# New places for the weight sums, sample rows by way of scratch, and a new order of issue in a two-part attention layer

## The chip, the cores and the metric

The kernel runs on one core of one Trainium2 chip. Its time is the device time of one execution in microseconds (us); the kernel before has a median of 773.05 us over three runs. One execution of it was also profiled, instruction by instruction, and that trace is what the text reads.

A core has five engines that run side by side, each with its own instruction queue in order: PE (TensorE, the matmuls; PEld is its weight load), DVE (VectorE), ACT (ScalarE), POOL (GpSimd) and SP (SyncE). In this kernel every transfer (DMA) is issued by SP.

## What is computed

One layer of a streaming encoder, in float32, for a prompt of 1024 frames and a sample of 32 frames that has 512 cached ones before it:

```python
hn = rmsnorm(h, g_pre)
qa, ka, va, ga, qb, kb, vb, gb = split(hn @ w_in)
oa = band_attention(qa, ka, va, bias)          # 8 heads x 64: softmax over a band of 576 frames
ob = stick_breaking(qb, kb, vb)                # 8 heads x 64: strictly causal, running products
y = concat(oa * silu(ga), ob * silu(gb)) @ w_out
h = h + rmsnorm(y, g_post)
h = h + sigmoid(h @ w_ple_gate) * (p @ w_ple)
```

Outputs are `h` of the prompt and of the sample, and the keys and values: of the prompt (the last 512 frames for A, all for B) and of the sample (32 frames x 8 heads x 64, four tensors: A keys, A values, B keys, B values).

## The kernel before, in words

**Work.** Each product takes its operands as a high and a low part in a rounded format, three matmuls for one. The heads go in pairs, in the order A0, B0, A1, B1, A2, B2, A3, B3 (number n = 0 to 7). Beside the attention of pair n (two heads of eight row blocks: scores, weights, transposed weights, product with the values) stand the projections q, k and v of pair n + 1, and beside the last pair all eight gate projections. Pairs n = 2, 3, 6 and 7 (A1, B1, A3, B3) also carry a sample attention over two pairs of heads (`with_sample`, `SAMPLE_AT`). Then come the small product `ple`, and the last two products, `w_out` and `w_ple_gate`. These two use a scheme of seven products of half-size blocks (`ORDER`) in place of eight, which needs sums of weight blocks.

**The sums.** `sum_weights(w, kt)` makes the sums for one of four slices of a weight: it loads four 128x512 blocks (tiles oB... for `w_out`, gB... for `w_ple_gate`, three buffers), makes four subtractions or additions in two halves each on POOL (8 instructions), and stores four results to `sum_dr`, a scratch tensor in DRAM. `SUMS_AT` says beside which pair two slices stand, `SUMS_STEP` after how many steps of that pair. The sums are read back from `sum_dr` when the attention is over.

**Sample rows.** `keys_out` transposes a pair's keys in 32x32 squares into a tile (ktA, ktB), and `values_out` does so for values (vtA, vtB). The sample's part of that tile is 128 x 32: four groups of 32 partitions, each holding 32 features of the 32 frames. `sample_rows` writes each group to the output with a transfer of its own: four for each pair's keys and four for its values, 64 in all, each of 32 runs of 128 bytes. For values the same tile also goes to the scratch `vs_dr[ab][p]` by `then(out, last)`; the sample attention reads its new values there (tile vn).

**The order.** Nothing is issued as it is written. A recorder collects all operations with their dependences, and `order` simulates the engines with costs from `cost`, finds for each operation how late it can be (`latest`, its due time), and simulates again with the due times as ranks; the instruction streams come out of that. The rank is `o.due + 10 * o.shift` (ns) in the last round. The shifts stand in two tables written out by hand: `AHEAD_OF` by engine and name of the written tile, `AHEAD_AT` by stage as well (pair n is stage n + 1). `PASSES` says how often due times and simulation are repeated. For SP, `ISSUE` is the time of an issue; `DMA_START`, `DMA_DONE`, `DMA_RATE`, `DMA_MARGIN` give a transfer's course. In `simulate`, SP may have 1900 pieces (rows of a transfer) under way (`AWAY`) and waits in the model when there would be more. `later` marks output transfers with a lower key, which counts in the first simulation alone. `rec.hold` keeps the buffers of a sum from being taken before the matmul that was recorded last.

All recorded operations have one line in the profile, L780, from which they are emitted; names of tiles tell them apart.

Of the kernel before, what the change touches and what calls it, by code (L numbers as in the profile page):

```python
# [10 lines left out]
AF = mybir.ActivationFunctionType  # L11
ALU = mybir.AluOpType

P = 128
D = 1024
SEQ = 1024
NS = 32
# [11 lines left out]
    ('ACT', 'L'): -809, ('ACT', 'Qfs'): -495, ('ACT', 'S'): -671, ('ACT', 'be'): 45,  # L29
    ('ACT', 'gT'): 1145, ('ACT', 'junk'): -1222, ('ACT', 'o'): 225, ('ACT', 'oT'): -1406,  # L30
    ('ACT', 'om'): -82, ('ACT', 'ot'): -967, ('ACT', 'p'): -874, ('ACT', 'pleo'): -1053,
    ('ACT', 'sgg'): 65, ('ACT', 'stq'): -314, ('ACT', 'stv'): -824, ('ACT', 'v'): 55,
    ('ACT', 'wTh'): -117, ('ACT', 'whS'): 246, ('ACT', 'whs'): 933, ('ACT', 'x'): -696,
    ('ACT', 'xS'): -616, ('DVE', 'Kl'): -588, ('DVE', 'L'): 544, ('DVE', 'S'): -85,
    ('DVE', 'Vl'): -913, ('DVE', 'cc'): -493, ('DVE', 'diags'): -1253, ('DVE', 'g'): 212,
    ('DVE', 'h'): -1097, ('DVE', 'hnl'): 570, ('DVE', 'lg'): 343, ('DVE', 'om'): -53,
    ('DVE', 'ot'): -267, ('DVE', 'over'): 483, ('DVE', 'sgg'): -356, ('DVE', 'sq'): 277,
    ('DVE', 'stats'): -1190, ('DVE', 'uu'): 246, ('DVE', 'v'): -653, ('DVE', 'vx'): -722,
    ('DVE', 'w'): -1469, ('DVE', 'wTl'): 37, ('DVE', 'wl'): 652, ('DVE', 'wlS'): -1002,
# [3 lines left out]
    ('POOL', 'be'): 196, ('POOL', 'gT'): 309, ('POOL', 'o'): -123, ('POOL', 'ogg'): 890,  # L43
    ('POOL', 'om'): 197, ('POOL', 'rs'): -497, ('POOL', 's'): -1046, ('POOL', 'sgg'): 929,
# [4 lines left out]
}  # L49
AHEAD_AT = {  # L50
    (0, 'ACT', 'pleo'): 1195, (0, 'ACT', 'sq'): 1380, (0, 'ACT', 'stk'): -1095, (0, 'ACT', 'v'): 1160,
    (0, 'DVE', 'hnl'): -45, (0, 'DVE', 'rb'): 799, (0, 'DVE', 'sq'): 461, (0, 'DVE', 'x'): 572,
# [3 lines left out]
    (2, 'ACT', 'be'): -135, (2, 'ACT', 'om'): 146, (2, 'ACT', 'stk'): -313, (2, 'ACT', 'stv'): 933,  # L56
    (2, 'ACT', 'v'): -818, (2, 'ACT', 'wTh'): 315, (2, 'ACT', 'wh'): -172, (2, 'DVE', 'S'): 534,
    (2, 'DVE', 'om'): 779, (2, 'DVE', 'wTl'): -209, (2, 'PE', 'PV'): 241, (2, 'PE', 'S'): 63,
    (2, 'PE', 'mm'): 48, (2, 'PE', 'ptw'): 89, (2, 'POOL', 'be'): -1200, (2, 'SP', 'kl'): 504,
    (2, 'SP', 'swap'): 262, (3, 'ACT', 'be'): 80, (3, 'ACT', 'om'): 256, (3, 'ACT', 'stk'): 956,  # L60
    (3, 'ACT', 'wh'): -21, (3, 'ACT', 'whs'): -356, (3, 'DVE', 'om'): -326, (3, 'DVE', 'ot'): -819,
# [3 lines left out]
    (4, 'ACT', 'om'): -35, (4, 'ACT', 'wTh'): -365, (4, 'ACT', 'whs'): -1064, (4, 'DVE', 'S'): -89,  # L65
    (4, 'DVE', 'Ss'): 1254, (4, 'DVE', 'ot'): 307, (4, 'DVE', 'wTl'): -134, (4, 'PE', 'S'): 77,
    (4, 'PE', 'ptw'): 56, (4, 'PE', 'ptws'): -349, (4, 'POOL', 'ksS'): -959, (4, 'POOL', 'om'): 162,
    (4, 'POOL', 'w'): -151, (4, 'POOL', 'wl'): 1076, (4, 'SP', 'Kcs'): 477, (4, 'SP', 'be'): -112,
    (4, 'SP', 'o'): -577, (4, 'SP', 'wr'): -890, (5, 'ACT', 'be'): -546, (5, 'ACT', 'kd'): -484,
    (5, 'ACT', 'stk'): 1450, (5, 'ACT', 'wTh'): -482, (5, 'DVE', 'S'): -110, (5, 'DVE', 'om'): -127,  # L70
# [3 lines left out]
    (6, 'ACT', 'L'): 734, (6, 'ACT', 'be'): -459, (6, 'ACT', 'kd'): 409, (6, 'ACT', 'stv'): 1412,  # L74
# [4 lines left out]
    (7, 'ACT', 'om'): 64, (7, 'ACT', 'stk'): -573, (7, 'ACT', 'wTh'): -208, (7, 'DVE', 'Kcs'): 660,  # L79
# [6 lines left out]
    (8, 'POOL', 'ogg'): -1077, (8, 'POOL', 'om'): 190, (8, 'POOL', 'sgg'): -350, (8, 'POOL', 'w'): 324,  # L86
# [3 lines left out]
    (10, 'POOL', 'r'): 153, (11, 'DVE', ''): -1125, (11, 'DVE', 'lg'): 155, (11, 'DVE', 'lo'): 1476,  # L90
    (11, 'DVE', 'ug'): -230, (11, 'DVE', 'wl'): -51, (11, 'DVE', 'wlS'): 1328, (11, 'POOL', 'h'): -525,
    (11, 'POOL', 'ms'): -252, (12, 'DVE', 'S'): 224, (12, 'DVE', 'cc'): 571, (12, 'POOL', 'gT'): -1069,
# [155 lines left out]
ISSUE = 550  # L248
TABLE = 1280
DMA_START, DMA_DONE, DMA_RATE, DMA_MARGIN = 1950, 300, 320.0, 2000  # L250
AWAY = 1900
# [4 lines left out]
PASSES = 1  # L256
# [158 lines left out]
class Recorder:  # L415
# [94 lines left out]
    def cost(eng, method, args, kw, writes, reads):  # L510
# [26 lines left out]
        size, run = 4, 0  # L537
        for v in (out, args[1]):
            if isinstance(v, View) and v.buf.pool is not None:
                size, run = 4 * v.shape[0] * v.free(), 4 * v.shape[-1]  # L540
# [82 lines left out]
    def simulate(self, rank):  # L623
# [83 lines left out]
        out, port, line, table, away, flying, last = [], 0.0, 0.0, AF.Exp, [], 0, 0.0  # L707
        while len(out) < len(self.ops):
# [26 lines left out]
            elif e == "SP":  # L735
                while away and (away[0][0] <= t or flying + o.pieces > AWAY):
                    landed, pieces = heapq.heappop(away)
                    flying -= pieces
                    t = max(t, landed)
                free[e] = t + o.busy  # L740
                line = max(line, t + DMA_START) + o.late
                heapq.heappush(away, (line + DMA_DONE, o.pieces))
                flying += o.pieces
                done = line + DMA_MARGIN
            else:
                if e == "ACT" and o.table not in (None, table):
                    t, table = t + TABLE, o.table
                if o.shared:
# [37 lines left out]
def stream_step(  # L786
# [235 lines left out]
    def sample_rows(dst, squares):  # L1022

        for g in range(4):
            later(dst[:, 32 * g:32 * g + 32], squares[32 * g:32 * g + 32])
# [1246 lines left out]
```

## Time and profile before

| | us |
|---|---|
| three runs: median (lowest to highest) | 773.05 (771.87 to 779.71) |
| the profiled execution | 773.43 |
| its span, from the first to the last instruction | 771.7 |
| PE busy | 758.4 |
| PEld busy | 698.9 |
| DVE, ACT, POOL busy | 611.6, 525.0, 447.2 |

The span is what the views cover; the profiled execution has 1.73 us around it. A matmul's record runs on while the next one has begun, so PE's busy time can hide short stops, and PEld's shows them. Rows of a view that lists instructions give the shortest, the median and the longest duration in ns, then the first and the last start. Rows of waits give the sum in us, how often, and the longest. Rows of the DMA list give KB each and the median us from issue to landing. Windows give the length of a stretch, the busy time of each engine in it with its count of instructions, the granted clock, the share of the time in which the DMA engines were busy, and GB/s.

### The profile page before, as it was taken

The numbers are of one execution on the slowest core, as the hardware profiler recorded it, in microseconds if no ns is written. First come the engines' busy times: TensorE is split into PE (matmuls) and PEld (weight loads), VectorE is DVE, ScalarE is ACT, GpSimd is POOL, SyncE is SP. The second block draws the span as 40 slices with busy tenths as digits, with TensorE's granted clock in tenths as the row PEclk, the third lists the DMA queues.
The fourth block names the chain that finished last, engine by engine and source line by source line (L and its number), as shares of the span: only waits on it lengthen the run. The fifth ranks groups of instructions, "written<-read, shape, count | busy, mean of one in ns | idle before, by whom it ended". The sixth has DMA issues, their size and how long they took to land.

```text
span 771.7 us, 14284 instructions
## 1 busy us (share of the span) xinstructions
PE 758.4 (98%) x4410; PEld 698.9 (91%) x4410; DVE 611.6 (79%) x1067; ACT 525.0 (68%) x1122; POOL 447.2 (58%) x503
## 2 busy tenths in 40 slices
PE   9999999999999999999999999999999999999997
PEld 7999999999989899999999999999998877888786
DVE  7837868878878898959898698698565688988965
ACT  6656776787766776866788586665347877884641
POOL 6624434751356682557874467679463448689533
PEclk9999999999999999999999999999999999999999
DMA  8658667476789858889799989897779866769664
GB/s 302 220 146 223 178 166 218 120 197 206 182 192 253 218 171 229 258 237 263 216 240 269 246 231 223 270 276 214 213 267 300 275 221 227 235 202 332 214 212 136
DMA packets 202333, 173.61 MB, mean 225 GB/s; under 512 B 66817, under 2 KB 164457, under 8 KB 202258
## 3 DMA queue, kind: packets, MB, share of 16 engines
q1 hardware_dynamic: 202258, 172.70, 77.1%
q8 instruction: 35, 0.57, 0.3%
q14 instruction: 40, 0.33, 0.1%
HBM read 105.46 MB, written 58.78 MB: 213 GB/s over the span
## 4 chain that ended last, share of the span: by engine, by line
PE 86%; DVE 4%; DMA 4%; SPq 3%; issue 1%; ACT 1%; DVEq 0%; POOL 0%; ACTq 0%; POOLq 0%
PE mm_gA L780 6%; PE mm_gB L780 6%; PE mm_kA L780 6%; PE mm_qA L780 5%; PE mm_kB L780 5%; PE mm_vA L780 5%; PE mm_qB L780 4%; PE PVB L780 4%; PE mm_vB L780 4%; PE SB L780 4%; PE PVA L780 3%; PE ple L780 3%; PE SA L780 3%; SPq L780 3%; PE g0P L780 3%; PE g2P L780 3%
## 5 line engine op out<-in xcount | busy, mean ns | idle before, releaser
L780 POOL TENSOR_TENSOR be<-be 128x128 f32<-128x128 f32 (+8 forms) x66 | 85.1, 1294 | 48.6 <-DVE be L780 23.0
L780 DVE TENSOR_TENSOR_SCAN be<-be,SB 128x384 f32<-128x384 f32 (+5 forms) x96 | 91.5, 963 | 8.2 <-ACT be L780 4.3
L780 ACT ACTIVATE be<-SB 128x384 f32<-128x384 f32 (+4 forms) x192 | 83.4, 497 | 18.2 <-DVE be L780 7.0
L780 DVE TENSOR_TENSOR wTl<-be,wTh 128x640 fp32r<-128x640 f32 (+2 forms) x48 | 51.9, 1086 | 11.2 <-ACT wTh L780 7.8
L780 ACT ACTIVATE be<-be,statA 128x640 f32<-128x640 f32 (+3 forms) x64 | 44.5, 696 | 11.6 <-DVE statA L780 11.5
L780 DVE STREAM_TRANSPOSE be<-be 128x640 f32<-128x640 f32 (+3 forms) x56 | 47.9, 866 | 3.4 <-POOL be L780 2.3
L780 ACT CAST wTh<-be 128x640 fp32r<-128x640 f32 (+2 forms) x48 | 37.6, 784 | 13.2 <-DMA be<-swapB 7.3
L780 PE MATMUL SB<-kdB,LB 128*128 128x384 f32 (+5 forms) x96 | 33.7, 354 | 0.4 <-issue 0.3
L780 PE MATMUL SB<-klB,LB 128*128 128x384 f32 (+5 forms) x96 | 33.3, 347 | 0.0
L780 DVE CUSTOM_DVE_ANT_0 be<-SA,biasA 128x320 f32<-128x320 f32 (+3 forms) x64 | 29.7, 481 | 4.4 <-PE SA L780 3.4
L780 POOL TENSOR_TENSOR gB<-gB,gB 128x256 f32<-128x256 f32 x32 | 26.9, 861 | 9.8 <-DMA gB<-in_w_ple_gate_dram 7.9
L780 ACT CAST wTh<-ptwB 128x512 fp32r<-128x512 f32 (+3 forms) x48 | 22.4, 484 | 13.0 <-PE PVB L780 8.0
L780 PE MATMUL SA<-kdA,LA 128*128 128x320 f32 (+2 forms) x96 | 30.3, 325 | 0.2 <-PE mm_kB L780 0.2
L780 PE MATMUL SA<-klA,LA 128*128 128x320 f32 (+2 forms) x96 | 30.1, 317 | 0.0
L780 POOL TENSOR_TENSOR oB<-oB,oB 128x256 f32<-128x256 f32 x32 | 25.6, 826 | 6.7 <-DMA oB<-in_w_out_dram 4.8
L780 PE MATMUL ptwB<-ident,be 128*128 128x128 f32 x144 | 26.5, 274 | 2.4 <-ACT be L780 1.0
L780 POOL TENSOR_TENSOR klB<-stkB,kdB 64x1024 fp32r<-64x1024 f32 x8 | 20.0, 2504 | 14.0 <-ACT kdB L780 12.1
L780 DVE TENSOR_TENSOR wTl<-ptwB,wTh 128x512 fp32r<-128x512 f32 (+3 forms) x48 | 25.0, 540 | 3.9 <-ACT wTh L780 3.7
L780 POOL TENSOR_TENSOR klA<-stkA,kdA 64x1024 fp32r<-64x1024 f32 (+2 forms) x9 | 19.3, 2150 | 14.4 <-ACT kdA L780 9.5
L780 DVE TENSOR_TENSOR wTl<-ptwA,wTh 128x128 fp32r<-128x128 f32 (+3 forms) x48 | 21.8, 478 | 5.3 <-ACT wTh L780 3.5
L780 DVE TENSOR_TENSOR LA<-stqA,LA 64x1024 fp32r<-64x1024 f32 (+2 forms) x9 | 15.6, 1730 | 11.9 <-ACT LA L780 11.8
L780 POOL TENSOR_TENSOR wl_vB<-wr_vB,wh_vB 128x512 fp32r<-128x512 f32 x8 | 10.5, 1309 | 24.5 <-DMA stvA<-swapA 13.3
(694 smaller groups left out, 2653.6 us busy)
## 6 DMA issues: line engine op xcount, KB each, us to landing
swapA<-be SPq DMA_DIRECT2D x24, 320.0 KB, 3.7
be<-swapA SPq DMA_DIRECT2D x96, 80.0 KB, 3.0
oB<-in_w_out_dram SPq DMA_DIRECT2D x16, 256.0 KB, 4.2
sum_dro<-oB SPq DMA_DIRECT2D x16, 256.0 KB, 3.2
gB<-in_w_ple_gate_dram SPq DMA_DIRECT2D x16, 256.0 KB, 3.9
sum_drg<-gB SPq DMA_DIRECT2D x16, 256.0 KB, 3.8
x<-in_x_prompt_dram SPq DMA_DIRECT2D x16, 256.0 KB, 3.9
h_dr<-h SPq DMA_DIRECT2D x8, 512.0 KB, 4.3
```

The lines of the kernel that those rows point to most:

```text
L780: getattr(getattr(tc.nc, o.what[0]), o.what[1])(*args, **kw)
```

## The change

It has three parts. The sums move from pairs 2, 4, 5, 6 to pairs 0, 1, 4, 5. The keys of the sample go to a scratch tensor `ks_dr` as the values already go to `vs_dr`, one transfer of 128 x 32 for each pair, and when the last pair (p == 3) of A or of B has been stored, one transfer from DRAM to DRAM moves all four pairs of the tensor to the output: four such transfers, for A and B keys and values. For values this now comes after the store to `vs_dr`. And the order is made with another model: at most eight transfers under way, other constants, the due times found in nine rounds, and all shifts in both tables new. `cost` now takes a size from a DRAM tensor if a transfer touches no tile. The two tables are left out here.

```diff
-ISSUE = 550
+ISSUE = 480
 TABLE = 1280
-DMA_START, DMA_DONE, DMA_RATE, DMA_MARGIN = 1950, 300, 320.0, 2000
-AWAY = 1900
+DMA_START, DMA_DONE, DMA_RATE, DMA_MARGIN = 1850, 1600, 320.0, 2100
+LANES = 8
...
-PASSES = 1
+PASSES = 9
...
-        for v in (out, args[1]):
-            if isinstance(v, View) and v.buf.pool is not None:
+        for v in (args[1], out):
+            if isinstance(v, View) and (v.buf.pool is not None or not run):
                 size, run = 4 * v.shape[0] * v.free(), 4 * v.shape[-1]
...
             elif e == "SP":
-                while away and (away[0][0] <= t or flying + o.pieces > AWAY):
-                    landed, pieces = heapq.heappop(away)
-                    flying -= pieces
-                    t = max(t, landed)
+                if len(landed) >= LANES:
+                    t = max(t, landed[-LANES])
                 free[e] = t + o.busy
                 line = max(line, t + DMA_START) + o.late
-                heapq.heappush(away, (line + DMA_DONE, o.pieces))
-                flying += o.pieces
+                landed.append(line + DMA_DONE)
                 done = line + DMA_MARGIN
...
+    ks_dr = {ab: scratch([4, P, NS], f"ks_dr{ab}") for ab in "AB"}
     vs_dr = {ab: scratch([4, P, NS], f"vs_dr{ab}") for ab in "AB"}
...
-    def sample_rows(dst, squares):
-
-        for g in range(4):
-            later(dst[:, 32 * g:32 * g + 32], squares[32 * g:32 * g + 32])
+    def sample_rows(ab, p, dst, squares, dr):
+
+        if squares is not None:
+            later(dr[p], squares)
+        if p == 3:
+            src = dr.rearrange("p (g t) f -> (p g) t f", t=32)
+            later(dst[0, 0].rearrange("t (p x) d -> t (p x d)", p=4).rearrange("t (x f) -> x t f", f=32), src)
...
-            sample_rows(o_s[0, 0, :, h2, :].rearrange("p h d -> p (h d)"), x[:, n:n + NS])
+            sample_rows(ab, p, o_s, x[:, n:n + NS], ks_dr[ab])
...
-            sample_rows(o_s[0, 0, :, h2, :].rearrange("p h d -> p (h d)"), last)
             then(out, last)
+            sample_rows(ab, p, o_s, None, vs_dr[ab])
...
-    SUMS_AT = {2: [('o', 0), ('o', 1)], 4: [('o', 2), ('o', 3)], 5: [('g', 0), ('g', 1)], 6: [('g', 2), ('g', 3)]}
+    SUMS_AT = {0:[('o',0),('o',1)],1:[('o',2),('o',3)],4:[('g',0),('g',1)],5:[('g',2),('g',3)]}
...
-    SUMS_STEP = {2: [10, 31], 4: [10, 26], 5: [7, 30], 6: [8, 28]}
+    SUMS_STEP = {0: [10, 31], 1: [10, 31], 4: [10, 26], 5: [7, 30]}
```

More of the change, by code (lines that the diff above doesn't have):

```diff
@@ L28 @@
 AHEAD_OF = {
[L29 to L39, printed above, removed]
[3 rows of a table removed]
-    ('POOL', 'be'): 196, ('POOL', 'gT'): 309, ('POOL', 'o'): -123, ('POOL', 'ogg'): 890,
@@ L44 @@
-    ('POOL', 'om'): 197, ('POOL', 'rs'): -497, ('POOL', 's'): -1046, ('POOL', 'sgg'): 929,
[4 rows of a table removed]
+    ('ACT', ''): -307, ('ACT', 'L'): -414, ('ACT', 'Qfs'): -110, ('ACT', 'Qhs'): -859,
+    ('ACT', 'S'): -381, ('ACT', 'be'): 32, ('ACT', 'g'): 244, ('ACT', 'gT'): -473,
+    ('ACT', 'hnh'): 1092, ('ACT', 'kd'): 363, ('ACT', 'newh'): -483, ('ACT', 'o'): -50,
+    ('ACT', 'om'): -5, ('ACT', 'p'): -1128, ('ACT', 'sq'): 108, ('ACT', 'stk'): 127,
+    ('ACT', 'stq'): -682, ('ACT', 'wh'): -79, ('ACT', 'whS'): -249, ('ACT', 'xS'): -955,
@@ new lines @@
+    ('ACT', 'xb'): -149, ('ACT', 'yb'): -199, ('DVE', ''): -1363, ('DVE', 'Kl'): 290,
+    ('DVE', 'L'): 377, ('DVE', 'R'): 818, ('DVE', 'S'): 18, ('DVE', 'Ss'): -133,
+    ('DVE', 'Vh'): -402, ('DVE', 'cc'): 216, ('DVE', 'diags'): -224, ('DVE', 'gT'): 610,
+    ('DVE', 'h'): 1157, ('DVE', 'hnl'): 253, ('DVE', 'lg'): -586, ('DVE', 'newl'): 326,
+    ('DVE', 'o'): 347, ('DVE', 'ot'): -72, ('DVE', 'over'): 1049, ('DVE', 'sgg'): 302,
[3 rows of a table added]
+    ('PE', 'ptxs'): 7, ('POOL', 'be'): 315, ('POOL', 'bias'): 960, ('POOL', 'g'): 573,
@@ L49 @@
+    ('POOL', 'ksS'): 1098, ('POOL', 'om'): -712, ('POOL', 'r'): -536, ('POOL', 'sgg'): 1213,
[5 rows of a table added]
 }
 AHEAD_AT = {
-    (0, 'ACT', 'pleo'): 1195, (0, 'ACT', 'sq'): 1380, (0, 'ACT', 'stk'): -1095, (0, 'ACT', 'v'): 1160,
-    (0, 'DVE', 'hnl'): -45, (0, 'DVE', 'rb'): 799, (0, 'DVE', 'sq'): 461, (0, 'DVE', 'x'): 572,
[3 rows of a table removed]
-    (2, 'ACT', 'be'): -135, (2, 'ACT', 'om'): 146, (2, 'ACT', 'stk'): -313, (2, 'ACT', 'stv'): 933,
-    (2, 'ACT', 'v'): -818, (2, 'ACT', 'wTh'): 315, (2, 'ACT', 'wh'): -172, (2, 'DVE', 'S'): 534,
@@ L58 @@
[L58 to L61, printed above, removed]
[3 rows of a table removed]
-    (4, 'ACT', 'om'): -35, (4, 'ACT', 'wTh'): -365, (4, 'ACT', 'whs'): -1064, (4, 'DVE', 'S'): -89,
-    (4, 'DVE', 'Ss'): 1254, (4, 'DVE', 'ot'): 307, (4, 'DVE', 'wTl'): -134, (4, 'PE', 'S'): 77,
@@ L67 @@
[L67 to L70, printed above, removed]
[3 rows of a table removed]
-    (6, 'ACT', 'L'): 734, (6, 'ACT', 'be'): -459, (6, 'ACT', 'kd'): 409, (6, 'ACT', 'stv'): 1412,
[4 rows of a table removed]
@@ L79 @@
-    (7, 'ACT', 'om'): 64, (7, 'ACT', 'stk'): -573, (7, 'ACT', 'wTh'): -208, (7, 'DVE', 'Kcs'): 660,
[6 rows of a table removed]
-    (8, 'POOL', 'ogg'): -1077, (8, 'POOL', 'om'): 190, (8, 'POOL', 'sgg'): -350, (8, 'POOL', 'w'): 324,
[3 rows of a table removed]
-    (10, 'POOL', 'r'): 153, (11, 'DVE', ''): -1125, (11, 'DVE', 'lg'): 155, (11, 'DVE', 'lo'): 1476,
-    (11, 'DVE', 'ug'): -230, (11, 'DVE', 'wl'): -51, (11, 'DVE', 'wlS'): 1328, (11, 'POOL', 'h'): -525,
-    (11, 'POOL', 'ms'): -252, (12, 'DVE', 'S'): 224, (12, 'DVE', 'cc'): 571, (12, 'POOL', 'gT'): -1069,
+    (0, 'ACT', 'hnh'): -902, (0, 'ACT', 'pleo'): 783, (0, 'ACT', 'sq'): 26, (0, 'ACT', 'v'): -215,
@@ new lines @@
+    (0, 'PE', 'mm'): -297, (0, 'PE', 'ple'): 252, (0, 'POOL', 'wl'): -634, (0, 'SP', 'wpr'): 528,
+    (0, 'SP', 'wr'): -232, (0, 'SP', 'x'): -74, (1, 'ACT', 'ot'): -442, (1, 'ACT', 'wTh'): 589,
+    (1, 'ACT', 'wh'): 43, (1, 'DVE', 'S'): 928, (1, 'DVE', 'om'): 258, (1, 'DVE', 'wTl'): 279,
+    (1, 'PE', 'S'): -86, (1, 'SP', 'sum'): -1097, (2, 'ACT', 'L'): 674, (2, 'ACT', 'be'): -112,
+    (2, 'ACT', 'ot'): -548, (2, 'ACT', 'vt'): 555, (2, 'ACT', 'wTh'): 152, (2, 'DVE', 'om'): 60,
+    (2, 'DVE', 'vt'): 389, (2, 'PE', 'S'): 43, (2, 'SP', 'o'): 677, (2, 'SP', 'sum'): 621,
@@ new lines @@
+    (3, 'ACT', 'Qfs'): 130, (3, 'ACT', 'stq'): 1238, (3, 'ACT', 'wh'): 323, (3, 'DVE', 'L'): -248,
+    (3, 'DVE', 'Vh'): 390, (3, 'DVE', 'Vl'): 233, (3, 'DVE', 'diags'): 564, (3, 'DVE', 'om'): 40,
+    (3, 'DVE', 'ot'): 169, (3, 'DVE', 'over'): 620, (3, 'DVE', 'vt'): 997, (3, 'DVE', 'vx'): 1005,
[3 rows of a table added]
+    (4, 'ACT', 'stq'): 92, (4, 'ACT', 'wTh'): -49, (4, 'DVE', 'Kl'): 168, (4, 'DVE', 'S'): 37,
+    (4, 'DVE', 'Vl'): 530, (4, 'DVE', 'newl'): -393, (4, 'DVE', 'om'): -78, (4, 'DVE', 'v'): 323,
[3 rows of a table added]
+    (5, 'ACT', 'stv'): 620, (5, 'ACT', 'wTh'): 828, (5, 'ACT', 'wh'): 111, (5, 'DVE', 'S'): 706,
[4 rows of a table added]
@@ new lines @@
+    (6, 'ACT', 'wTh'): 110, (6, 'ACT', 'wh'): 247, (6, 'DVE', 'S'): -173, (6, 'DVE', 'om'): -161,
+    (6, 'DVE', 'ot'): 125, (6, 'PE', 'S'): -71, (6, 'PE', 'mm'): -119, (6, 'SP', 'be'): -1228,
+    (6, 'SP', 'g'): 487, (6, 'SP', 'sum'): 117, (6, 'SP', 'swap'): -830, (6, 'SP', 'wr'): 687,
+    (7, 'ACT', 'be'): 447, (7, 'ACT', 'kd'): -699, (7, 'ACT', 'om'): -1093, (7, 'ACT', 'stv'): -159,
+    (7, 'ACT', 'wTh'): 220, (7, 'ACT', 'wh'): 657, (7, 'DVE', 'stats'): 251, (7, 'DVE', 'wTl'): 52,
[4 rows of a table added]
+    (8, 'ACT', 'om'): -708, (8, 'ACT', 'ot'): -106, (8, 'ACT', 'sgg'): -442, (8, 'ACT', 'wTh'): 312,
@@ new lines @@
+    (8, 'DVE', 'Kcs'): -163, (8, 'DVE', 'Kl'): 236, (8, 'DVE', 'S'): 304, (8, 'DVE', 'Vl'): 1322,
[3 rows of a table added]
+    (8, 'SP', 'wr'): 210, (9, 'ACT', ''): 132, (9, 'ACT', 'ple'): -857, (9, 'ACT', 'x'): 1236,
+    (9, 'SP', 'ple'): 1191, (10, 'ACT', ''): 229, (10, 'ACT', 'S'): -140, (10, 'ACT', 'junk'): -1187,
+    (10, 'ACT', 'wh'): -393, (10, 'ACT', 'whS'): -503, (10, 'ACT', 'wl'): 21, (10, 'ACT', 'x'): -316,
+    (10, 'ACT', 'xb'): -346, (10, 'PE', 'o'): 176, (10, 'POOL', 'h'): 1495, (10, 'SP', 'x'): -820,
@@ L93 @@
+    (11, 'ACT', 'g'): 533, (11, 'ACT', 'junk'): 705, (11, 'ACT', 'x'): 430, (11, 'ACT', 'xS'): 262,
+    (11, 'DVE', 'h'): -403, (11, 'PE', 'o'): -12, (12, 'ACT', 'gT'): -495, (12, 'ACT', 'x'): -260,
+    (12, 'DVE', 'gT'): -1415, (12, 'DVE', 'gj'): 887, (12, 'POOL', 's'): -859, (12, 'SP', 'hh'): 748,
+    (13, 'ACT', 'x'): -379, (13, 'DVE', 'S'): 55, (13, 'DVE', 'cc'): 684, (13, 'DVE', 'wlS'): -69,
+    (13, 'PE', 'g'): 217,
 }
@@ L705, in leave @@
                 come(new.place, b.gone)
-        out, port, line, table, away, flying, last = [], 0.0, 0.0, AF.Exp, [], 0, 0.0
+        out, port, line, table, landed, last = [], 0.0, 0.0, AF.Exp, [], 0.0
         while len(out) < len(self.ops):
```

54 rows, old and new, of tables (AHEAD_AT, AHEAD_OF) are left out of this document.

## The prediction

> **What bounds the kernel now.** I read four views in this order: the page's totals with its chain, the windows by pair of heads, PE's and SP's waits, and SP's own timeline at one place where PE stood still.
>
> ```profile
> span 771.7 us, 14284 instructions
> PE 758.4 (98%) x4410; PEld 698.9 (91%) x4410; DVE 611.6 (79%) x1067; ACT 525.0 (68%) x1122; POOL 447.2 (58%) x503
> PE 86%; DVE 4%; DMA 4%; SPq 3%; issue 1%; ACT 1%; DVEq 0%; POOL 0%; ACTq 0%; POOLq 0%
> ```
>
> PE is busy for 98% of the span, and 86% of the chain that ended last is PE. The change touches no matmul, so it can only win back time in which PE waits: 771.7 - 758.4 = 13.3 us by this row. The granted clock is 1.00 in every window below, so no gain waits there.
>
> The windows are cut where the value products of the pairs end, so 64 to 554 holds the eight pairs A0, B0, A1, B1, A2, B2, A3, B3 in this order; 554 to 583 is the rest of the gates. The columns after PE are PEld, DVE, ACT and POOL, then the clock, the DMA share and GB/s.
>
> ```profile
> 64.00:118.00 54.00, 54.00 (x351) 52.99 (x350) 41.58 (x94) 39.81 (x88) 19.37 (x27) 1.00 0.72 195
> 118.00:180.00 62.00, 61.88 (x386) 59.48 (x385) 52.94 (x92) 46.03 (x100) 31.92 (x31) 1.00 0.63 173
> 180.00:240.00 60.00, 58.82 (x377) 56.25 (x377) 50.25 (x108) 43.45 (x102) 28.85 (x37) 1.00 0.78 202
> 240.00:309.00 69.00, 67.68 (x425) 64.38 (x424) 59.06 (x108) 50.32 (x110) 39.00 (x43) 1.00 0.79 218
> 309.00:357.00 48.00, 46.22 (x294) 43.99 (x293) 38.83 (x78) 37.20 (x84) 29.55 (x39) 1.00 0.86 248
> 357.00:416.00 59.00, 58.47 (x368) 56.41 (x367) 52.63 (x88) 43.62 (x93) 43.55 (x45) 1.00 0.88 239
> 416.00:479.00 63.00, 61.18 (x392) 58.64 (x392) 51.52 (x110) 45.52 (x103) 36.90 (x49) 1.00 0.91 243
> 479.00:554.00 75.00, 75.00 (x475) 73.44 (x474) 58.68 (x89) 42.48 (x95) 55.12 (x59) 1.00 0.85 242
> ```
>
> PE's idle time in these eight rows is 0.00, 0.12, 1.18, 1.32, 1.78, 0.53, 1.82 and 0.00 us, 6.75 us together. The other half of the 13.3 us lies ahead of 64 and in the tail, which the change leaves alone. A second measure is finer, because a short stop disappears inside PE's overlapping records: the weight load, which precedes every matmul. It stands still for 1.01, 2.52, 3.75, 4.62, 4.01, 2.59, 4.36 and 1.56 us, 24.4 us in 490. The last row shows the same kind of work running without any PE gap and still loses 1.56 of 75, or 2.1%; 2.1% of 490 is 10.3 us. So some 24.4 - 10.3 = 14.1 us can be won, pair by pair -0.1, 1.2, 2.5, 3.2, 3.0, 1.4, 3.0 and 0. That is my ceiling for a gain: 773 - 14 = 759.
>
> **The change, part by part.** First, where the sums run now and what they cost. The lines on oB and gB are their loads, subtractions and stores; the two window answers show POOL's part alone.
>
> ```profile
> L780 POOL TENSOR_TENSOR gB<-gB,gB 128x256 f32<-128x256 f32 x32 | 26.9, 861 | 9.8 <-DMA gB<-in_w_ple_gate_dram 7.9
> L780 POOL TENSOR_TENSOR oB<-oB,oB 128x256 f32<-128x256 f32 x32 | 25.6, 826 | 6.7 <-DMA oB<-in_w_out_dram 4.8
> L780 SPq DMA_DIRECT2D oB<-in_w_out_dram x16: 342/430/627, 182.2 to 356.1; - x16
> L780 SPq DMA_DIRECT2D sum_dro<-oB x16: 319/432/987, 208.7 to 365.1; - x16
> L780 SPq DMA_DIRECT2D woT<-sum_dro x8: 326/430/676, 563.9 to 587.9; - x8
> 180.00:240.00 60.00, 0.00 (x0) 0.00 (x0) 0.00 (x0) 0.00 (x0) 4.36 (x6) 1.00 0.78 202
> 240.00:309.00 69.00, 0.00 (x0) 0.00 (x0) 0.00 (x0) 0.00 (x0) 8.27 (x10) 1.00 0.79 218
> 416.00:479.00 63.00, 0.00 (x0) 0.00 (x0) 0.00 (x0) 0.00 (x0) 14.72 (x18) 1.00 0.91 243
> ```
>
> Each of the four places takes two slices of a weight, which is 16 subtractions on POOL (16 x 0.84 = 13.4 us), 8 loads and 8 stores on SP (16 x 0.43 = 6.9 us of its queue). The amount stays; the places change from pairs 2, 4, 5, 6 to 0, 1, 4, 5. Pairs 2 and 6 (A1 and A3) also carry sample attention, and so do 3 and 7; 0 and 1 carry none.
>
> What pairs A1 to B1 and A3 get back: they lose 2.5, 3.2 and 3.0 us by the list above, 8.7 together, with 6, 10 and 18 of the subtractions inside them. The ends are 0 (sample attention alone makes the loss) and 8.7. At A3 the trace lets me see how much a sum matters.
>
> ```profile
> 435.45 0.63 SPq L780 DMA_DIRECT2D wr_vB<-in_w_in_dram  x1
> 436.18 0.46 SPq L780 DMA_DIRECT2D sum_drg<-gB  x1
> 436.68 0.42 SPq L780 DMA_DIRECT2D out_dram<-vtA  x1
> 437.20 0.96 SPq L780 DMA_DIRECT2D vnsA<-vs_drA  x2
> 437.67 5.12 DMA vnsA<-vs_drA
> 442.86 0.41 ACT newh L780
> PE ptwA L780 <- DVE statA L780: 1.3, 1, 1.3
> ```
>
> The first four lines are SP's queue, the next two the chain, the last PE's longest wait (it stands at 444.30). A sum's store and a value store go out just ahead of the sample's new values; these then take 5.12 us to land, on the chain, and PE stops soon after. Without the sum the load leaves 0.46 us earlier, or about a third of that 1.3 us wait. I take a third of 8.7 us: -2.9.
>
> What A0 and B0 pay: POOL rises from 19.37 to 32.8 us of 54 and from 31.92 to 45.3 of 62, 61% and 73%; B3 runs at 55.12 of 75, 73%, with no PE gap, so POOL as such has cover. DMA adds 16 x 0.25 = 4 MB to each, some 75 GB/s: 195 and 173 become about 270 and 245, near the 248 of the A2 row. The lower end is 0; the upper is that both windows fall to A2's loss of 3.0 us in place of -0.1 and 1.2, which is +4.9. I take a quarter, +1.2, since neither pair has sample attention. If POOL's cover goes, B0's keys (kl, a POOL subtraction) come late, and with them the scores that PE runs next.
>
> Second, the sample rows. The counts below hold prompt rows too (16 each for keys, 4 for values); 16 in each are sample rows.
>
> ```profile
> L780 SPq DMA_DIRECT2D out_dram<-ktA x32: 322/485/1853, 56.1 to 395.2; - x32
> L780 SPq DMA_DIRECT2D out_dram<-ktB x32: 332/530/905, 90.4 to 508.9; - x32
> L780 SPq DMA_DIRECT2D out_dram<-vtA x20: 347/424/897, 75.1 to 436.7; - x20
> L780 SPq DMA_DIRECT2D out_dram<-vtB x20: 331/490/1617, 117.3 to 532.9; - x20
> L780 SPq DMA_DIRECT2D vs_drB<-vtB x4: 319/372/572, 124.1 to 510.2; - x4
> out_dram<-vtB SPq DMA_DIRECT2D x16, 4.0 KB, 3.7
> ```
>
> 64 issues of about 0.48 us go, 30.7 us of SP's queue. In their place come 8 stores of keys into scratch and 4 transfers, 12 x 0.42 = 5.0 us. SP gets 25.7 us back, 3.3% of the span. SP holds 3% of the chain, 23 us; 3.3% of this is 0.8. The ends are 0 (nobody waits for an output) and 23; I take -0.8, because these rows are the kernel's least urgent and mostly fill holes. The value transfers read scratch that has just been written: if one is issued right behind its store, SP stands for a landing, 3.7 us by the last line, and all behind it (loads of the next weights, attention's swaps) stand too. Four times that is +15 us; taken at 0, since only the transfers of the last A and the last B pair can do it and other ready transfers can go between.
>
> A page speaks against this part: by the Trainium skill, DMA: Bandwidth & Descriptors, section Specifications, transfers under 512 B are read-modify-writes, and the new way cuts the scratch copy as well as the output into 128-byte runs, 3072 of them for 2048. At the same page's 10.5 ns a packet (section Bandwidth), doubled, the 1024 more are 1.3 us over 16 engines, an estimate, and the sum would be -2.2 us. No run here shows the price of such a run by itself; by the landing row above a 4 KB transfer, cut into such runs, lands no later than others.
>
> Third, the order. Every rank is formed anew: nine rounds of due times in place of one, two new tables of shifts (a unit is 10 ns), other transfer constants, and eight transfers under way in place of 1900 pieces. No row prices this. What bears on it are SP's waits for landings and its longest wait:
>
> ```profile
> SPq L780 <- DMA x<-in_x_prompt_dram: 2.6, 3, 1.0
> ...
> SPq L780 <- DMA oggB<-o_dr: 0.2, 1, 0.2
> SPq L780 <- ACT kdA L780: 10.7, 2, 10.3
> ```
>
> SP waits for landings in 33 such groups between those two, about 30 us in all. An order that expects them would put work for PE in the holes. The ends are -11 (the 14.1 us less the 2.9 already counted) and +10.3 for one more wait like the last line. I take -1.0, near zero, because both ends are as far and only a small part of SP's waits reaches PE now.
>
> The sum: -2.9 + 1.2 - 0.8 - 1.0 = -3.5 us. The profiled execution took 773.43 us (span 771.7 and 1.73 around it), 0.38 over the median of 773.05; from the median that gives 769.5, and I write 769.
>
> **The rivals.** (a) Clearly faster. The weight-load reading is right, and an order that fits what SP can have under way closes most of the holes: 10 of the 14.1 us, 763. For it: the eight windows show 24.4 us against PE's 6.75. Against: three rows of the eight are near their floor already. The Trainium skill says the same in Perfetto Trace Analysis, section Identifying the Most-Contended Engine, where matmul busy time is no good measure of headroom and weight-load busy time is; the trace agrees in so far as the two differ, 91% against 98%.
>
> (b) Slower, by one mechanism: SP is a single queue in order, and the new ranks put a transfer whose data is late ahead of the swaps on which PE's next transposed weights depend. The price is the wait that exists once already, 10.3 us: 773 + 10.3 = 783. It decides once the stop is longer than the projection matmuls that PE has at hand; in the trace the 10.3 us on kdA did not reach PE, whose longest wait is 1.3. Two of them would give 794.
>
> (c) The sums don't go where it says. Their results are first read at 563.9, so their due times are late, and SP takes them when it is otherwise free; they ran from 182 to 365 where they were written beside pairs 2 and 4. They then stay beside samples, and only the -0.8 is left: 772.
>
> (d) The sums do go to A0 and B0 and cost there the full 4.9, with nothing won: 778.
>
> **How the numbers follow.** About 1%, or 7.7 us, is what a measurement of this kernel tells from no change. My forecast of 769 gets 0.27 (its own range 765 to 775), (c) 0.06, (d) 0.05: together 0.38 within 1%. (a) gets 0.32, as a second, finer measure shows the room and nothing is added to PE. (b) gets 0.30, as all of SP's order is new and one queue carries every transfer. The range goes from 758, a little past the ceiling of 759, to 788, which takes in one stop of 10.3 us with the cost of (d).
>
> **What would show it.** POOL's subtractions on oB between 64 and 180, and PE's idle time in the A1 and A3 windows under 0.6 us each: the first term. PE idle over 0.5 us in A0 or B0: the second. 52 fewer issues on SP and SPq under 3% of the chain: the third. PEld's standstill from A0 to B3 well under 24 us: the order, (a); a single PE wait over 3 us behind a swap: (b). The forecast is wrong if a PE wait of that kind appears, or if PE's idle time falls while the weight loads stand still as before.

## The result and the profile after

The kernel after takes 768.65 us (median of nine runs, 767.52 to 771.65), the kernel before 773.08 in the same comparison. The ratio is 0.9931 with a 95% interval from 0.9911 to 0.9952, so 3.7 to 6.9 us are gone. The profiled execution took 767.52 us, its span is 765.7. Ratios below are always to the kernel before on the same chip; I turn them into us with 773.1. The ratios are those on record, and the quotient of two medians can differ a little from them: here 768.65 / 773.08 is 0.9943, or 4.4 us.

The page's totals, and the chain by engine:

```profile
span 765.7 us, 14211 instructions
PE 755.8 (99%) x4410; PEld 699.5 (91%) x4410; DVE 615.7 (80%) x1067; ACT 525.1 (69%) x1122; POOL 447.7 (58%) x503
PE 86%; DMA 5%; DVE 3%; ACT 2%; issue 1%; SPq 1%; POOL 0%; ACTq 0%; DVEq 0%; POOLq 0%
```

The same 4410 matmuls; PE's idle time falls from 13.3 to 765.7 - 755.8 = 9.9 us, and its busy time by 2.6 us; the work is the same, so these are probably stops too short to appear between two overlapping records. SPq on the chain falls from 3% to 1%. The windows, cut where the value products of A0 to B3 end in this run:

```profile
64.00:117.00 53.00, 52.47 (x340) 51.37 (x339) 42.85 (x89) 37.42 (x82) 19.10 (x29) 1.00 0.84 220
117.00:181.00 64.00, 64.00 (x397) 61.42 (x396) 56.81 (x98) 48.79 (x105) 43.91 (x47) 1.00 0.82 224
181.00:247.00 66.00, 64.42 (x415) 62.09 (x414) 55.71 (x114) 47.29 (x107) 34.94 (x47) 1.00 0.82 218
247.00:308.00 61.00, 60.10 (x382) 57.72 (x381) 55.90 (x98) 46.86 (x102) 31.76 (x33) 1.00 0.75 201
308.00:360.00 52.00, 51.53 (x329) 49.71 (x328) 46.74 (x89) 39.37 (x89) 33.26 (x40) 1.00 0.88 253
360.00:412.00 52.00, 52.00 (x325) 50.21 (x325) 46.66 (x78) 42.75 (x90) 34.78 (x37) 1.00 0.82 212
412.00:479.00 67.00, 66.88 (x433) 64.99 (x432) 57.32 (x119) 49.60 (x110) 37.28 (x44) 1.00 0.89 229
479.00:548.00 69.00, 69.00 (x438) 67.50 (x438) 52.41 (x84) 38.63 (x88) 51.85 (x54) 1.00 0.83 228
```

A0 to B3 took 490 us and take 484: the whole difference of the two spans lies here. PE's idle time in the eight windows is 0.53, 0, 1.58, 0.90, 0.47, 0, 0.12 and 0, together 3.60 us where it was 6.75. The weight load's standstill is 1.63, 2.58, 3.91, 3.28, 2.29, 1.79, 2.01 and 1.50, together 19.0 us where it was 24.4. Pair by pair the standstill changes by +0.6, +0.1, +0.2, -1.3, -1.7, -0.8, -2.4 and -0.1. A1, where I looked for the first gain, has none, and its PE idle time is 1.58 us where the prediction's sign asked for under 0.6. A likely reason stands in the windows of the sums' tile oB alone, where POOL's subtractions are counted:

```profile
64.00:117.00 53.00, 0.00 (x0) 0.00 (x0) 0.00 (x0) 0.00 (x0) 4.39 (x6) 1.00 0.84 220
117.00:181.00 64.00, 0.00 (x0) 0.00 (x0) 0.00 (x0) 0.00 (x0) 10.47 (x12) 1.00 0.82 224
181.00:247.00 66.00, 0.00 (x0) 0.00 (x0) 0.00 (x0) 0.00 (x0) 9.95 (x12) 1.00 0.82 218
247.00:308.00 61.00, 0.00 (x0) 0.00 (x0) 0.00 (x0) 0.00 (x0) 1.45 (x2) 1.00 0.75 201
```

Written beside A0 and B0, 14 of the 32 run beside A1 and B1. So rival (c) is half right: the sums drift behind the pairs that they are written beside.

SP stands longer for landings than before, not shorter: the waits of SP that a landing ended add up to 39.6 us where they were 31.4. Two of them are new, for the stores of the sample's keys:

```profile
SPq L781 <- DMA ks_drA<-ktA: 3.1, 1, 3.1
SPq L781 <- DMA ks_drB<-ktB: 1.1, 1, 1.1
```

### The profile page after: what moved, and what is told of

It reads as the page before. It is cut to its first block, busy times and chain, and to the rows that moved or that the text cites. A ratio compares the mean times of both kernels' runs of the same rounds, so it can differ in the third digit from the quotient of the medians.

```text
span 765.7 us, 14211 instructions
## 1 busy us (share of the span) xinstructions
PE 755.8 (99%) x4410; PEld 699.5 (91%) x4410; DVE 615.7 (80%) x1067; ACT 525.1 (69%) x1122; POOL 447.7 (58%) x503
## 2 busy tenths in 40 slices
DMA packets 202525, 173.73 MB, mean 227 GB/s; under 512 B 67009, under 2 KB 164649, under 8 KB 202450
## 4 chain that ended last, share of the span: by engine, by line
PE 86%; DMA 5%; DVE 3%; ACT 2%; issue 1%; SPq 1%; POOL 0%; ACTq 0%; DVEq 0%; POOLq 0%
PE mm_vA L781 6%; PE mm_kB L781 6%; PE mm_qA L781 6%; PE mm_gA L781 6%; PE mm_gB L781 6%; PE mm_kA L781 6%; PE mm_qB L781 5%; PE PVB L781 4%; PE SA L781 3%; PE ple L781 3%; PE SB L781 3%; PE PVA L781 3%; PE o3P L781 3%; PE o1P L781 3%; PE g1P L781 3%; PE g0P L781 3%
## 5 line engine op out<-in xcount | busy, mean ns | idle before, releaser
L781 POOL TENSOR_TENSOR be<-be 128x256 f32<-128x256 f32 (+8 forms) x66 | 84.7, 1290 | 47.6 <-ACT be L781 17.8
L781 ACT ACTIVATE be<-SB 128x384 f32<-128x384 f32 (+5 forms) x192 | 85.2, 499 | 18.2 <-DVE be L781 9.1
L781 DVE TENSOR_TENSOR wTl<-be,wTh 128x640 fp32r<-128x640 f32 (+2 forms) x48 | 58.6, 1228 | 4.5 <-ACT wTh L781 3.6
L781 DVE CUSTOM_DVE_ANT_0 be<-SA,biasA 128x320 f32<-128x320 f32 (+2 forms) x64 | 29.4, 481 | 4.0 <-PE SA L781 3.1
L781 POOL TENSOR_TENSOR h<-h,x 128x512 f32<-128x512 f32 (+1 forms) x18 | 23.4, 1320 | 1.3 <-DVE h L781 1.3
L781 PE MATMUL PVB<-wTh,v2B 128*128 128x512 f32 (+1 forms) x96 | 24.1, 344 | 0.0
```

Of the source, the lines that this page charges most:

```text
L781: getattr(getattr(tc.nc, o.what[0]), o.what[1])(*args, **kw)
```

## The experiments

The theory to test was the sum of the prediction: sums -1.7, rows -0.8, order -1.0. The main rivals were that the new order alone made the gain, or that the work alone did. To part work from order I needed kernels in which one changes and the other doesn't. In those called "order kept", the planner runs on the work of the kernel named and gives its sequence, and only the named operations are dropped, replaced or put elsewhere as the sequence is issued.

**1. The sums moved, order kept.** In `emit`, the sums' operations are shifted in simulated time by the distance between the pairs and merged back by time.

```diff
-        ops = self.order()
+        ops = self.moved(self.order())
...
+    BACK = {('o', 0): ('A1', 'A0'), ('o', 1): ('A1', 'A0'), ('o', 2): ('A2', 'B0'), ('o', 3): ('A2', 'B0'), ('g', 0): ('B2', 'A2'), ('g', 1): ('B2', 'A2'), ('g', 2): ('A3', 'B2'), ('g', 3): ('A3', 'B2')}
```

> The kernel before with its order kept instruction for instruction; only the 192 operations of the weight sums (and the buffers they take) are put earlier in that order, from beside A1, A2, B2, A3 to beside A0, B0, A2, B2. Theory 1 (the terms of the prediction: sums -2.9 + 1.2): 771.4 us, between 770 and 772.5. Rival (the new order alone made the gain): 773 or slower, as the sums have cover in both places. Rival (d) of the prediction (A0 and B0 pay 4.9): 776 to 778.

Measured: 810.59 us, ratio 1.0472 [1.0449, 1.0495]. Neither theory expected that. The waits of PE, the window around the longest one, and SP's queue in it:

```profile
PE PVA L805 <- DVE v2A L805: 22.5, 1, 22.5
```

```profile
192.00:215.00 23.00, 0.87 (x6) 0.57 (x4) 1.25 (x3) 2.04 (x3) 6.74 (x9) 0.63 0.56 163
215.00:219.00 4.00, 3.60 (x14) 3.41 (x15) 3.27 (x8) 3.18 (x11) 0.61 (x3) 0.56 0.65 177
219.00:223.00 4.00, 4.00 (x27) 3.98 (x27) 3.31 (x7) 3.29 (x8) 0.34 (x2) 1.00 0.94 288
```

```profile
180.33 2.26 SPq L805 DMA_DIRECT2D oB<-in_w_out_dram  x3
188.56 1.71 SPq L805 DMA_DIRECT2D sum_dro<-oB  x3
190.72 0.33 SPq L805 DMA_DIRECT2D oB<-in_w_out_dram  x1
195.20 0.32 SPq L805 DMA_DIRECT2D sum_dro<-oB  x1
195.57 2.04 SPq L805 DMA_DIRECT2D oB<-in_w_out_dram  x3
201.52 3.04 SPq L805 DMA_DIRECT2D sum_dro<-oB  x3
...
208.33 1.78 SPq L805 DMA_DIRECT2D stvA<-swapA  x4
```

The slices of A1 and A2 ran into each other here, and the sums became a ladder: three loads, a wait for POOL, three stores, and the next load waits until a buffer is stored. SP is one queue, so the values that come back from scratch (stvA) leave at 208, after 28 us in which SP issues sums and waits between them, with seven other transfers at the end, and PE's value product waits 22.5 us for v2A. This is rival (b)'s mechanism, made by hand. The product stood next in PE's queue, and projection matmuls did not fill the wait: of one group of eight, two ran at 192.38 and the other six at 217.81, behind the product.

**2. The sums moved in two blocks, order kept.** One shift for all of w_out, one for w_ple_gate, so that nothing crowds.

```diff
-        ops = self.order()
+        ops = self.moved(self.order())
...
+    BACK = {('o', 0): ('A1', 'A0'), ('o', 1): ('A1', 'A0'), ('o', 2): ('A1', 'A0'), ('o', 3): ('A1', 'A0'), ('g', 0): ('B2', 'A2'), ('g', 1): ('B2', 'A2'), ('g', 2): ('B2', 'A2'), ('g', 3): ('B2', 'A2')}
```

> The kernel before, its order kept, the sums' operations put earlier again, but with one shift for all of w_out (from A1's start to A0's) and one for all of w_ple_gate (from B2's to A2's), so that no four slices crowd together and they stand about where the kernel after has them (82 to 261 and 307 to 444). Theory (the sums' place is worth the 1.4 us by which the two runs without sums differ): 771.5, between 770.5 and 773. Rival (a place that the order was not made for always costs): 776 or more.

Measured: 782.43 us, ratio 1.0117 [1.0089, 1.0144], +9 us. All but the last two of the w_out subtractions, which start at 325 us, stand about where the kernel after has them, and still it costs: the rival was right. In this order the place of the sums can't be judged apart from the order of everything around them.

**3 and 4. No sums at all, order kept.** The sums' operations are left out, and the last two products read plain blocks of the weights in transfers of the same size, so the sums are not computed and these products are not the layer's. The kernel after has the same edit in its own order.

```diff
+        for o in rec.ops[first:]:
+            o.skip = o.eng != "CTL"
```

> The kernel before with its order kept, but the weight sums left out: no loads, no subtractions, no stores for them, and the last two products read plain weight blocks where the sums stood, by transfers of the same size; so the output is not the reference's. It bounds what any place of the sums can win. Theory 1: 768 to 770 (about a third to a half of the 8.7 us that A1, B1 and A3 lose). Rival (order alone): 772 to 773.

Measured: 767.62 us, ratio 0.9918 [0.9899, 0.9937], so the sums cost the kernel before 6.3 us.

> The kernel after with its own order kept and the sums left out in the same way. Theory 1 (the sums cost less at their new places): at most 1.2 us under the kernel after, 767.4 to 768.6. Rival (the sums cost as much as before, and the gain is the order's): as far below 768.6 as the kernel before without sums is below 773.1.

Measured: 763.64 us, ratio 0.9866 [0.9842, 0.9890]; against the kernel after, 0.9866 / 0.9931 = 0.9935, or 5.0 us. The first theory, at most 1.2 us for the sums at their new places, missed; the rival's reading, that they cost about as much as before, is nearer. The new places save about 6.3 - 5.0 = 1.3 us, but the two costs are uncertain by some 1.5 and 2.5 us, so this difference is not clear of zero: a saving by the new places is not shown.

**5. The rows by way of scratch, order kept.** The first of four key-row transfers becomes the store, the last one of pair 3 the transfer from DRAM to DRAM.

```diff
+            if len(seen) == 1 and store:
+                tc.nc.sync.dma_start(dr.get()[p], squares.get())
+            if len(seen) == 4 and p == 3:
+                tc.nc.sync.dma_start(whole..., src)
```

> The kernel before with its order kept; the first of each four key-row transfers becomes the store to scratch, the other rows fall away, and the last of the four of pair 3 becomes the transfer from DRAM to DRAM: 64 issues become 12. Theory 1 (term -0.8): 772.3 us. Rival (order alone): 773.1, no change. If SP's issue time is what PE waits for, up to 23 us could go: below 765. If the value transfers hold SP up: 775 or more.

Measured: 771.16 us, ratio 0.9959 [0.9943, 0.9976]: -3.2 us (-1.9 to -4.4), where I had -0.8. The chain of its page and two windows (B2 and A3), to be set against those of before:

```profile
PE 93%; DVE 2%; SPq 1%; issue 1%; DMA 1%; ACT 1%; POOL 0%; DVEq 0%; ACTq 0%
357.00:416.00 59.00, 59.00 (x374) 57.29 (x373) 52.81 (x91) 44.53 (x96) 42.95 (x46) 1.00 0.89 243
416.00:479.00 63.00, 62.94 (x403) 60.54 (x403) 52.65 (x110) 45.93 (x102) 38.48 (x51) 1.00 0.94 248
```

PE's idle time at B2 goes from 0.53 to 0, at A3 from 1.82 to 0.06, and the chain is 93% PE for 86%.

**6. Only A3's value rows later, order kept.** Four transfers are put behind the sample's loads that they stood ahead of; 64 issues remain.

```diff
+        rows = [o for o in ops if o in self.rows]
+        last = [n for n, o in enumerate(ops) if o.eng == "SP" and isinstance(o.args[0], View) and o.args[0].buf.name == "vnsA1"][-1]
+        ops = [o for o in ops[:last + 1] if o not in rows] + rows + [o for o in ops[last + 1:] if o not in rows]
...
+                rec.rows = rec.ops[-4:]
```

> The kernel before, its order kept, but the four transfers of A3's value rows put right behind the loads of the sample's new values, ahead of which they stood; nothing else changes, 64 issues stay. Theory (what the rows cost is that they stand ahead of urgent loads at A3): half or more of the 3.1 us, 770.5 to 771.7. Rival (SP's issue time as a sum, wherever it falls): 773.1.

Measured: 773.92 us, ratio 0.9999 [0.9978, 1.0020]: nothing. The windows show where PE's time went:

```profile
416.00:479.00 63.00, 62.27 (x403) 60.39 (x402) 53.49 (x113) 45.76 (x104) 37.45 (x50) 1.00 0.92 246
479.00:554.00 75.00, 72.97 (x456) 70.36 (x455) 55.33 (x87) 41.70 (x93) 52.03 (x58) 1.00 0.84 231
```

At A3 PE's idle time shrinks from 1.82 to 0.73 us, as the theory wanted. Then B3, which had none, gets 2.03. Its stops begin at 482 us, some 45 us after the four issues, and I did not trace whether the four cause them. Experiments 5 and 6 say together that the price of the rows is not the wait that these four precede at A3; that their number counts in this queue is the likely reading, and not shown.

**7. The rows straight again in the kernel after, order kept.** Each store of keys becomes four transfers, each store of values is followed by its four, and the four transfers from DRAM to DRAM fall away.

```diff
+            for g in range(4):
+                tc.nc.sync.dma_start(rows[:, 32 * g:32 * g + 32], x.get()[32 * g:32 * g + 32])
...
```

> The kernel after, its order kept; each store to scratch of key rows becomes four transfers straight to the output, each store of new values is followed by its four, and the four transfers from DRAM to DRAM fall away: 12 issues become 64 again. Theory (52 issues on SP cost about 3 us in any order): 771 to 773. Rival (they cost only where the order before had them, ahead of A3's loads): 768.6 to 769.6.

Measured: 782.74 us, ratio 1.0122 [1.0086, 1.0157], which is 1.9% over the kernel after. Both theories missed: this is far more than 3 us. But the four transfers stand in one block here, at a place made for one, so it is no measure of their price.

**8. Both work parts, order kept** (2 and 5 together).

> Both: that spread move of the sums and the rows by way of scratch, in the order of the kernel before. Theory (work explains all, the new order nothing): 773.1 - 3.1 - 1.4 = 768.6, the time of the kernel after. Rival (the new order carries part of the gain): 770 or more.

Measured: 779.89 us, ratio 1.0084 [1.0054, 1.0114]. Against experiment 2 the rows bring 0.33%, 2.6 us, the same as in 5 within the intervals, though not clear of zero here. The theory that work alone makes the kernel after is wrong: in the order of before, the moved sums cost more than the rows bring.

**9 to 12. Ranked anew.** Both tables of shifts empty, in either kernel; then the third part of the change alone; then the first two alone.

```diff
-AHEAD_OF = {...}
-AHEAD_AT = {...}
+AHEAD_OF, AHEAD_AT = {}, {}
```

> The kernel before, ranked anew with both tables of shifts empty; the work is the same. Theory (each table is fitted to its own work and carries a gain of its own size): clearly slower, 785 to 810. Rival (due times alone give the order, shifts are small change): 773 to 778.

> The kernel after with both tables empty: new work, nine rounds of due times, eight transfers under way. If the better model of SP is what gains, this beats the kernel before without shifts by 4 us or more; if the tables are what counts, the two differ by chance, within some 10 us either way, and both stand well above 773.

> The kernel after with the sums beside 2, 4, 5, 6 and the rows straight to the output as before: the third part of the change alone. Theory (a table serves the work that it was made with): slower than both, 775 to 795. Rival (the new model and tables are better by themselves): 770 to 772.

> The kernel before with the new places of the sums and the rows by way of scratch, ranked by the old model and the old tables: the first two parts alone. Theory: slower than both, 775 to 795, although its work is the cheaper by some 4 us. Rival (the work explains all): 768 to 770.

| planner | work | tables | ratio to before (95%) |
|---|---|---|---|
| old | old | old: the kernel before | 1 |
| old | old | none | 1.0088 [1.0057, 1.0119] |
| new | new | none | 0.9920 [0.9889, 0.9950] |
| new | new | new: the kernel after | 0.9931 [0.9911, 0.9952] |
| new | old | new | 1.0349 [1.0330, 1.0369] |
| old | new | old | 1.0140 [1.0119, 1.0162] |

Three things follow. The new tables bring nothing that shows: without them the new kernel is as fast. The old tables are worth 0.88%, 6.8 us, with the old work, and both mixes of a table with work that it was not made for are slower than either kernel with its own: 1.0140 is slower even than the old planner without any table. That the table does this, and not the planner, was not separated: neither mix was run with empty tables. And without tables the new planner with the new work beats the old with the old by 0.9920 / 1.0088 = 0.983, some 13 us. The third part alone came out above the range expected for it, the first two alone within theirs, and the kernel before without tables between its two; the kernel after without tables did what was expected if the better model of SP is what gains.

Part of these prices is the granted clock. In the run of the old planner with old work and no tables it falls to 0.50 for three stretches of some 3.4 us; here are one of them and the stretch behind it:

```profile
95.40:98.70 3.30, 3.30 (x14) 3.20 (x13) 1.53 (x4) 0.79 (x3) 0.00 (x0) 0.50 0.42 140
98.80:102.10 3.30, 3.30 (x22) 3.30 (x22) 0.43 (x1) 0.83 (x2) 0.10 (x1) 1.00 0.72 210
```

In the profiles of the kernels before and after the clock falls nowhere before the last microsecond. By estimate, at half speed, the three stretches are 3 x 3.4 / 2 = 5.1 of the 9.2 us by which that profile is longer than before's. So the 6.8 and the 13 us are not prices of waits alone.

## Why the prediction was right, point by point

The time, the sign and the range held: 769 was forecast, 768.65 came. The terms were less good than their sum, and that it was met within half a microsecond is in part luck: by the ratio 5.3 us are gone, where the terms add up to 3.5, and the rows alone are off by 2.4.

**The ceiling.** PE's idle time from A0 to B3 did fall by nearly half, and nothing outside these windows moved. Of the 14.1 us that I read from the weight load, 5.4 came. As a measure of lost time the weight load's standstill must be read for one kind of matmul only. In the window of the products after the attention the kernel after shows

```profile
577.00:676.00 99.00, 99.00 (x432) 78.39 (x431) 76.53 (x110) 76.68 (x159) 57.60 (x58) 1.00 0.76 247
```

and in that of the gate projections before it, with matmuls of 352 columns,

```profile
548.00:577.00 29.00, 29.00 (x183) 29.00 (x182) 14.60 (x24) 11.57 (x23) 14.39 (x13) 1.00 0.83 268
```

PE has no gap in either, but the weight load rests for 20.6 us of 99 in the first, where nearly all matmuls have 512 columns, and not at all in the second. One load takes 0.19 us; 99 us over 432 matmuls are 0.23 each. So "24.4 against 6.75" was weak evidence for rival (a), and the rule of the Trainium skill (Perfetto Trace Analysis, Identifying the Most-Contended Engine) that weight-load time shows the headroom doesn't hold in such a window.

**What A1 to B1 and A3 get back (-2.9), what A0 and B0 pay (+1.2).** The net of -1.7 fits the 1.3 us between experiments 3 and 4, which don't exclude that it is nothing. The places were wrong in part: A1 gave nothing, and 12 subtractions went on running there; A3 and B1 gave 3.7 us of standstill; A0 and B0 paid 0.7. A2 and B2, which I had not counted, gave 2.5. These windows hold the rows and the new order too, so none of it is the sums' alone. "POOL as such has cover" held: B0's window has 43.91 of 64 us on POOL and PE doesn't stop. How much the sums' price hangs on the order around them was not in the prediction; experiments 1 and 2 show it with +37 and +9 us for the same work.

**The sample rows (-0.8).** This is the mis-sized term: -3.2 us in experiment 5. I took the share of the chain that SP holds (3%) as the price of SP's time, and called the rows fill for holes. Experiment 6 tried one explanation, the place of four of them at A3, and it brought nothing. What I feared of the value transfers, that SP stands for the landing of the store just before, happened to the keys, which I had not thought of: SP waits 3.1 and 1.1 us for the two stores (ks_drA, ks_drB). It cost nothing that shows, as PE is busy for all of the window 360 to 412 that holds the longer wait. The two value transfers leave 4.0 and 6.6 us after the stores that they read, and SP doesn't stop for them. The new issues are each slower than I had it, a median of 0.60 and 0.79 us for the key stores in place of 0.42, which is little beside 52 fewer. The estimate for short runs from the Trainium skill's figure (DMA: Bandwidth & Descriptors, Bandwidth), +1.3 us of DMA time, was not to be seen in the time either: the four transfers of 512 runs of 128 bytes landed after 2.3 to 4.6 us, within what other transfers take. The profile's pages count 66817 packets under 512 bytes before and 67009 after, only 192 more; that fits 1024 more runs less 16 small packets for each of the 52 transfers that went.

```profile
ks_drA<-ktA SPq DMA_DIRECT2D x4, 16.0 KB, 3.4
out_dram<-ks_drA SPq DMA_DIRECT2D x1, 64.0 KB, 2.3
out_dram<-vs_drB SPq DMA_DIRECT2D x1, 64.0 KB, 4.6
```

**The order (-1.0).** Of the 5.3 us, 5.3 - 3.2 - 1.3 = 0.8 are left for it, a remainder that carries the errors of all three. So the size is not contradicted, and that is all; the reason may be one that I had not seen, two large amounts that cancel. By the table, the old tables' 6.8 us are given up. Without tables the new kernel is 13 us better than the old; rows and sums explain 3.2 + 1.3 = 4.5 of it, which leaves some 8 for the planner (eight under way, nine rounds, other constants). That last number is a difference between runs with different work, one of them with falls of the clock, and so only argued. Which of the planner's edits makes it was not tried; the new planner on the old work without tables would be the run to settle it. The way that I gave, an order that expects SP's waits for landings and puts work for PE in the holes, fits what the profile after shows, SP's waits for landings up from 31.4 to 39.6 us and PE's idle time down from 13.3 to 9.9; but no run shows which part of the change did it.

**The rivals.** (a) did not happen. (b) did not happen to this change: PE's longest wait is 1.3 us, as before, although SP again has one wait of 10.0 us (for ktA). Its mechanism is real, and it can cost more than I gave: a stop of 22.5 us in experiment 1. (d) is excluded by the windows of A0 and B0.

## What to carry to other kernels

Where one in-order queue issues every transfer, don't price an issue by the queue's share of the chain, and don't expect to win back a wait by moving the issue that stands ahead of it: here dropping 52 of 970 issues was worth 3.2 us where the share gave 0.8, and moving four was worth nothing. A hand-made table of priorities is part of the work that it was fitted to: when the work changes, compare with the table empty before you trust it. And when two parts of a change can only be had with a new order, try each in the old order with everything else held, and expect the moved part to look worse than it is.

## What the runs showed of the hardware

A stop of PE can cost more than its length. After the 22.5 us wait in experiment 1 the granted clock is 0.56 for the next four microseconds and 1.00 after that (the three windows there), and over that whole run PE needs 766.4 us for the matmuls that take 758.4 in the kernel before. PE is busy for 12 us at a clock of 0.50 in that run, in three stretches, so by estimate some 6 of these 8 us are the clock's. The third part of the change alone shows the same: 769.6 us.

```profile
PE 766.4 (95%) x4410; PEld 705.4 (87%) x4410; DVE 611.8 (76%) x1067; ACT 524.6 (65%) x1122; POOL 446.4 (55%) x503
```

```profile
PE 769.6 (96%) x4410; PEld 704.9 (88%) x4410; DVE 614.1 (77%) x1067; ACT 525.8 (66%) x1122; POOL 447.9 (56%) x503
```

The Trainium skill puts the stop of PE that lets the clock fall to half at over some 3.4 us (TensorE: Matmul & The Clock Gate, HAM oscillation); the windows agree for the 22.5 us stop. But shorter ones do it here too. In the run of the third part alone PE waits 2.3 us from 477.0 on:

```profile
476.90:479.40 2.50, 0.23 (x2) 0.17 (x2) 2.39 (x4) 1.50 (x4) 1.77 (x3) 1.00 0.97 237
479.50:482.80 3.30, 3.30 (x14) 3.21 (x14) 2.52 (x6) 2.85 (x8) 3.30 (x5) 0.50 1.03 286
482.90:486.20 3.30, 3.30 (x23) 3.28 (x23) 3.19 (x5) 1.56 (x4) 2.04 (x2) 1.00 1.07 271
```

At 0.50 PE gets through 14 matmuls in 3.3 us, and through 23 right after. Yet in experiment 7 a wait of 2.3 us too, at 272.7, is followed by no fall (22 matmuls in the next 3.4 us at 1.00). So the length of one stop doesn't settle it, and what does was not tried.

"Eight under way" is what these programs do. In the records of the kernel before, SP's transfers signal eight semaphores in turn. For the five of them whose completions are all recorded, none of 601 transfers was issued before the one eight earlier had landed; the closest came 16 ns after it, and 36 within 100 ns. So it looks as if a slow landing can hold up a transfer that has nothing to do with it, which no experiment here tried by itself. A planner that counts pieces doesn't know of such a limit.
